# Summing the first modulation on TensorE, applying it ahead of the transposes, and writing the position bias behind the last token tile

## The chip, the cores and the metric

The kernel runs on one core of a Trainium2 chip. The metric is the device time of one execution in microseconds (us). An execution of one kernel is also taken with a hardware profiler, and every row below comes from that one profiled execution. The engines are TensorE (PE in the profile; PEld is its weight load), VectorE (DVE), ScalarE (ACT), GpSimd (POOL) and SyncE (SP), whose queue issues nearly all DMAs of this kernel.

## What is computed

One transformer layer for 1024 tokens of width 1024 in float32, with a mixer of two attention groups and a mixture of experts. The part that the change touches is the beginning of the mixer:

```python
c_act = jax.nn.silu(c)
mod = c_act @ w_ada[l] + b_ada[l]
shift_m, scale_m, gate_m, shift_f, scale_f, gate_f = jnp.split(mod, 6, axis=-1)
h = modulate(rms_norm(x), shift_m, scale_m)      # rms_norm(x) * (1 + scale_m) + shift_m
proj = h @ w_in[l]
qa, ka, va, qb, kb, vb = jnp.split(proj, ...)
qa, ka = apply_partial_rope(qa), apply_partial_rope(ka)
oa = windowed_gqa_sink(qa, ka, va, sink[l])
ob = neighbourhood_attn(qb, kb, vb, rpb[l])      # rpb: learned 2-D relative position bias
```

Everything behind it (both attentions, the output projection, the router, the experts and the final norm) is the same in both kernels.

## The kernel before, in words

All of this stands in `proj_and_a`. Tokens are worked in eight tiles of 128. A projection needs the modulated tokens with the features on the partitions, split into a high and a low part (`hh`, `hl`, fp32r) so that three matmuls (`mm3`, lines 236 to 238) give nearly float32 accuracy.

The first block (lines 336 to 404) does this:

- SyncE issues the DMAs in an order written out by hand (lines 337 to 355): the conditioning vector and the whole modulation bias into `cb`, then x tiles (`xt`, two buffers, line 350) mixed with eight blocks of `w_ada` of 1 MB each (`wa`, three buffers, line 345), the weights of keys and values (`w_chunk(512)`, whose load is line 516), the position bias (`bias_tables`, lines 655 to 664) and the rotary table `ropet` (line 355). A DMA that needs a buffer waits on SyncE until the buffer is free, and everything behind it waits too.
- `bias_tables` loads `rpb` into `erow` (line 661), negates it on POOL (line 662) and writes it 64 times over into the DRAM tensor `d_b` (line 663), whence the second attention group reads it later (line 674).
- Each x tile is squared and summed on ACT (line 366), scaled by its inverse root mean square on VectorE (line 369), transposed on TensorE (line 373) and copied by ACT into `xT` (line 375), not yet modulated.
- The modulation is summed on VectorE: for each of four column blocks, eight steps (lines 385 and 387) multiply rows of `w_ada` by the value of the conditioning vector and add them up over `acc`; TensorE then adds over the partitions (line 389), which gives scale and shift as columns `scol` (lines 392, 394).
- The modulated `hh` is written by ACT (line 399), the same in full precision by VectorE (line 400), and their difference `hl` by VectorE or POOL (line 401), in five spans of tokens, one instruction for each of eight feature blocks.
- `keys_values(i)` projects tile i onto keys and values (24 matmuls), copies them (lines 327, 329), applies the rotary table on POOL (`rope_op`, lines 533 to 536) and transposes the keys of the tile before (`k_turn`, line 317).

Behind the block come the mask (line 409), the sinks (line 411), the query weights (`w_chunk(0)`), and then query projections and windowed attention, with other projections filled in. On all engines but SyncE within this block, the order of instructions is set by a planner that places them by its own estimates of times. A tile of memory that is used again waits for the last reader of what lay there.

Of the kernel before, what the change touches and what calls it, by code (L numbers as in the profile page):

```python
# [5 lines left out]
F32 = mybir.dt.float32  # L6
# [3 lines left out]
AF = mybir.ActivationFunctionType  # L10
ALU = mybir.AluOpType
# [4 lines left out]
D = 1024  # L16
S = 1024
NT = 8
KD = 8
# [207 lines left out]
class Kernel:  # L227
# [64 lines left out]
    def proj_and_a(self):  # L292
        tc, nc = self.tc, self.nc
        V, A, P, T = nc.vector, nc.scalar, nc.gpsimd, nc.tensor
        with (
# [7 lines left out]
            scol = hp.tile([128, 16], F32, name="scol")  # L303
            ccol = hp.tile([128, 8], F32, name="ccol")
            bcol = hp.tile([128, 48], F32, name="bcol")
            self.hh, self.hl, self.kp, self.chunks = hh, hl, kp, 0
            kh = kp.tile([128, 2, S], F32R, name="kh")
            kl = kp.tile([128, 2, S], F32R, name="kl")
# [24 lines left out]
                    k_turn(i - 1)  # L333

            with tc.tile_pool(name="xp", bufs=1) as xp, tc.manual_schedule(engines={mybir.EngineType.SP}):
                cb = xp.tile([56, 128], F32, name="cb")
                nc.sync.dma_start(cb[0:8], self.c.rearrange("a (k p) -> (a k) p", p=128))
                nc.sync.dma_start(cb[8:56], self.b_ada.rearrange("a (k p) -> (a k) p", p=128))
                xt, wts = {}, {}
                for z in "0,1,w0,w1,2,w4,3,w5,4,w2,5,w3,w6,w7,6,7".split(","):  # L340
                    if z[0] == "w":
                        n = int(z[1:])
                        c, kk = divmod(n, 2)
                        w = wts[n] = xp.tile([128, 4, 512], F32, name="wa", bufs=3)
                        nc.sync.dma_start(w, self.w_ada[0, kk * 512:(kk + 1) * 512, c * 512:(c + 1) * 512]
                                          .rearrange("(k p) n -> p k n", p=128))
# [4 lines left out]
                wkv = self.w_chunk(512)  # L351
                with tc.issue_after(self.loaded):
                    self.bias_tables()
                self.ropet = kp.tile([128, NT, 32], F32, name="ropet")
                nc.sync.dma_start(self.ropet, self.rope)
                pc = ps.tile([128, 512], F32, name="pm", bufs=3)
                T.transpose(pc[:, 0:56], cb, self.idt[:56, :56])
# [3 lines left out]
                V.tensor_copy(bcol, pc[:, 8:56])  # L361
                xT = xp.tile([128, KD, S], F32, name="xT")
                for i in range(NT):
                    st = xp.tile([128, 2], F32, name="st", bufs=4)
                    junk = xp.tile([128, D], F32, name="junk", bufs=1)
                    A.activation(junk, xt[i], AF.Square, accum_out=st[:, 0:1])
                    A.activation(st[:, 1:2], st[:, 0:1], AF.Sqrt, bias=self.eps, scale=1.0 / D)
                    V.reciprocal(st[:, 1:2], st[:, 1:2])
                    V.tensor_scalar(junk, xt[i], st[:, 1:2], None, op0=ALU.mult)
                    for m in range(2):  # L370
                        pt = ps.tile([128, 512], F32, name="psc")
                        for k in range(4):
                            T.transpose(pt[:, k * 128:(k + 1) * 128], junk[:, (4 * m + k) * 128:(4 * m + k + 1) * 128],
                                        self.idt)
                        A.activation(xT[:, 4 * m:4 * m + 4, i * 128:(i + 1) * 128],
                                     pt.rearrange("p (k t) -> p k t", k=4), AF.Copy)
                pc = ps.tile([128, 512], F32, name="pm", bufs=3)
                pcv = pc[:, 0:32].rearrange("p (j t) -> p j t", t=2)
                for half in range(2):
                    for c in (half, half + 2):  # L380
                        acc = xp.tile([128, 512], F32, name="acc", bufs=2)
                        for k in range(KD):
                            w = wts[2 * c + k // 4][:, k % 4, :]
                            if k == 0:
                                V.tensor_scalar(acc, w, ccol[:, 0:1], None, op0=ALU.mult)
                            else:
                                V.scalar_tensor_tensor(acc, w, ccol[:, k:k + 1], acc, op0=ALU.mult, op1=ALU.add)
                        for j in range(4 * c, 4 * c + 4):
                            T.matmul(pc[:, 2 * j:2 * j + 2], acc[:, (j % 4) * 128:(j % 4 + 1) * 128],
                                     self.ones[:, 0:2], start=True, stop=True)  # L390
                    js = slice(4 * half, 4 * half + 4)
                    V.tensor_tensor(scol[:, js], pcv[:, js, 0], bcol[:, js], op=ALU.add)
                    js = slice(8 + 4 * half, 12 + 4 * half)
                    V.scalar_tensor_tensor(scol[:, js], pcv[:, js, 0], 1.0, bcol[:, js], op0=ALU.add, op1=ALU.add)
                for t0, t1 in ((0, 128), (128, 256), (256, 512), (512, 768), (768, 1024)):
                    for k in range(KD):
                        sl = slice(t0, t1)
                        x = xT[:, k, sl]
                        A.activation(hh[:, k, sl], x, AF.Identity, scale=scol[:, 8 + k:9 + k], bias=scol[:, k:k + 1])
                        V.tensor_scalar(x, x, scol[:, 8 + k:9 + k], scol[:, k:k + 1], op0=ALU.mult, op1=ALU.add)  # L400
                        (P if k % 4 > 1 else V).tensor_tensor(hl[:, k, sl], x, hh[:, k, sl].bitcast(F32),
                                                              op=ALU.subtract)
                    for i in range(t0 // 128, t1 // 128):
                        keys_values(i)
# [247 lines left out]

    def bias_tables(self):


        nc = self.nc
        e = self.kp.tile([120, 128], F32, name="erow", bufs=1)
# [3 lines left out]
        nc.sync.dma_start(self.d_b.rearrange("h (c m) -> h c m", m=128),  # L663
                          e.rearrange("h (c m) -> h c m", c=1).to_broadcast([120, 64, 128]))

    def tables(self, pool, h, mc, mi):

# [1076 lines left out]
```

## Time and profile before

| | |
|---|---|
| three timed runs, us | 2292.54, 2292.58, 2282.31 (median 2292.54) |
| the profiled execution's own time, us | 2281.06 |
| its span, first to last instruction, us | 2279.3 |
| mean granted TensorE clock | 0.968 |
| TensorE busy | 2083.8 us, 91% of the span |
| VectorE busy | 1593.2 us, 70% |
| ScalarE busy | 967.3 us, 42% |
| GpSimd busy | 1112.3 us, 49% |

The span is 1.8 us shorter than the time of the execution. Busy shares are means over stages with different limits. The granted clock is given as a share of full speed (2.4 GHz). A matmul's row gives its duration from issue to its modelled end; matmuls are pipelined, so the distance from one start to the next says what one costs in a row of them.

### The profile page before, as it was taken

To read this page: it belongs to the slowest core of one execution; us is meant where nothing else is said; L and a number is where in the kernel's file an instruction comes from. 1 tells how busy PE (TensorE), PEld (TensorE's weight loads), DVE (VectorE), ACT (ScalarE), POOL (GpSimd) and SP (SyncE) were. 2 spreads that over 40 slices of the span, in tenths; PEclk is the share of its full clock that TensorE was granted. 3 is DMA by queue.
4 is the path that set the end of the run, shared out by engine and by line. 5 is a ranking of instruction groups with operands and counts; after the bars stand their busy time and mean duration, and the time that the engine had idled before them with its cause. 6 is when DMAs were issued, how large, how long until landed. Compare 5 with 4: busy or idle time off the path is not lost. (4 is left out here: it accounts for less than half of the span.)

```text
span 2279.3 us, 34822 instructions
## 1 busy us (share of the span) xinstructions
PE 2083.8 (91%) x12050; PEld 1551.4 (68%) x12050; DVE 1593.2 (70%) x2860; ACT 967.3 (42%) x1650; POOL 1112.3 (49%) x970
## 2 busy tenths in 40 slices
PE   4799999999978898988979999999999999999983
PEld 4688777777767876665546555566687777877772
DVE  7577645876577599888875454455686878878864
ACT  5343335764353456554653121222233434444553
POOL 1522122543556467778784234333536455556453
PEclk9899999999988999999999999999999999999987
DMA  7755486924466698898979998999898999888775
GB/s 254 183 154 163 139 222 176 203 66 143 120 191 184 207 306 293 299 287 259 314 241 355 376 321 291 341 348 331 264 341 279 328 299 315 303 282 301 267 231 187
DMA packets 328243, 579.20 MB, mean 254 GB/s; under 512 B 40021, under 2 KB 78149, under 8 KB 326729
## 3 DMA queue, kind: packets, MB, share of 16 engines
q1 hardware_dynamic: 304657, 524.23, 67.4%
q0 software_dynamic: 23408, 52.71, 11.1%
q8 instruction: 97, 1.59, 0.3%
q14 instruction: 81, 0.66, 0.1%
HBM read 518.25 MB, written 58.92 MB: 253 GB/s over the span
## 5 line engine op out<-in xcount | busy, mean ns | idle before, releaser
L1309 POOL TENSOR_TENSOR w<-w,w 128x288 fp32r<-128x288 f32 x456 | 595.2, 1364 | 544.3 <-ACT w L1307 518.9
L1307 ACT ACTIVATE w<-w 128x1024 fp32r<-128x1024 f32 x456 | 469.6, 1054 | 517.1 <-PE accH L1536 119.3
L1309 DVE TENSOR_TENSOR w<-w,w 128x736 fp32r<-128x736 f32 x456 | 506.6, 1124 | 202.4 <-ACT w L1307 200.4
L1536 PE MATMUL accH<-xH,w 128*128 128x256 f32 (+9 forms) x1408 | 400.3, 296 | 2.7 <-POOL w L1309 1.8
L1534 PE MATMUL accH<-xH,w 128*128 128x256 f32 (+6 forms) x1024 | 322.0, 318 | 1.7 <-ACT xH L243 0.6
L1535 PE MATMUL accH<-xH,w 128*128 128x256 f32 (+6 forms) x1024 | 316.9, 311 | 0.3 <-DVE xH L244 0.3
L1536 PEld LDWEIGHTS accH<-xH,w 128*128 128x128 f32 x1408 | 272.1, 195 | 15.4 <-issue 5.0
L1534 PEld LDWEIGHTS accH<-xH,w 128*128 128x128 f32 x1024 | 194.5, 191 | 49.8 <-issue 27.3
L1535 PEld LDWEIGHTS accH<-xH,w 128*128 128x128 f32 x1024 | 195.4, 191 | 5.3 <-DVE xH L244 0.7
L1559 PE MATMUL accL<-w,xL 128*32 128x512 f32 (+3 forms) x896 | 176.9, 599 | 0.8 <-issue 0.8
L236 PE MATMUL accH<-w,hH 128*128 128x512 f32 (+3 forms) x368 | 150.0, 410 | 2.8 <-ACT w L1307 2.8
L237 PE MATMUL accH<-w,hH 128*128 128x512 f32 (+3 forms) x368 | 147.1, 400 | 0.0
L238 PE MATMUL accH<-w,hH 128*128 128x512 f32 (+3 forms) x368 | 143.0, 401 | 3.4 <-POOL w L1309 2.3
L238 PE MATMUL accL<-w,xL 128*72 128x512 f32 (+4 forms) x256 | 106.2, 415 | 38.5 <-POOL w L1309 28.4
L1532 PE MATMUL accH<-xH,w 128*128 128x416 f32 (+2 forms) x384 | 116.2, 378 | 10.7 <-DVE t L1424 10.6
L1492 POOL DMA_INDIRECT d_y<-y,lsH x54 | 96.7, 1791 | 47.3 <-DVE y L1486 33.1
L236 PE MATMUL accL<-w,xL 128*72 128x512 f32 (+4 forms) x256 | 104.0, 406 | 1.8 <-ACT w L1307 1.5
L1451 DVE TENSOR_TENSOR t<-accL,biasL 32x512 f32<-32x512 f32 (+8 forms) x88 | 60.5, 688 | 62.1 <-PE accL L1559 46.7
L237 PE MATMUL accL<-w,xL 128*72 128x512 f32 (+4 forms) x256 | 103.5, 404 | 0.0
L236 PEld LDWEIGHTS accH<-w,hH 128*128 128x128 f32 (+3 forms) x368 | 68.3, 186 | 49.9 <-issue 19.2
L1559 PEld LDWEIGHTS accL<-w,xL 128*32 128x32 f32 (+3 forms) x896 | 39.5, 115 | 84.0 <-issue 79.3
L236 PE MATMUL pm<-whi,hh 128*128 128x256 f32 x320 | 93.0, 291 | 2.4 <-DVE va L329 1.2
(362 smaller groups left out, 4477.0 us busy)
## 6 DMA issues: line engine op xcount, KB each, us to landing
w<-in_w_gate_up SPq DMA_DIRECT2D x264, 1024.0 KB
w<-in_w_down SPq DMA_DIRECT2D x132, 1024.0 KB
aw<-in_w_ada SPq DMA_DIRECT2D x64, 256.0 KB
wraw<-in_w_in SPq DMA_DIRECT2D x18, 512.0 KB
xt<-in_x SPq DMA_DIRECT2D x16, 512.0 KB
wa<-in_w_ada SPq DMA_DIRECT2D x8, 1024.0 KB
d_h<-zero SPq DMA_DIRECT2D x9, 512.0 KB
d_y<-zero SPq DMA_DIRECT2D x18, 256.0 KB
```

What stands on the lines that cost most here:

```text
L236: mm(ps, lh, rh, start=start, stop=False)
L237: mm(ps, ll, rh, start=False, stop=False)
L238: return mm(ps, lh, rl, start=False, stop=stop).ins
L1307: A.activation(hi, w, AF.Copy)
L1309: eng.tensor_tensor(lo[:, :, cs], w[:, :, cs], hi[:, :, cs].bitcast(F32), op=ALU.subtract)
L1451: V.tensor_tensor(t, p[o:o + nt], bv[o:o + nt], op=ALU.add)
L1492: s = P.indirect_dma_start(out=self.d_y[c], out_offset=bass.IndirectOffsetOnAxis(ap=b["ls"][:nt, 0:1], axis=0), in_=y, in_offset=None, com ...
L1532: mm(p[:, :2 * sp], hi[:, k, ws], x[:, :, kk, :], start=kk == 0, stop=False)
L1534: mm(p[:, :sp], hi[:, k, ws], x[:, 0, kk, :], start=kk == 0, stop=False)
L1535: mm(p[:, :sp], hi[:, k, ws], x[:, 1, kk, :], start=False, stop=False)
L1536: mm(p[:, :sp], lo[:, k, ws], x[:, 0, kk, :], start=False, stop=kk == 7)
L1559: mm(p[o:o + nt], w[:, kk, :], hi[:, k, :], start=kk < len(at), stop=kk >= 8 - len(at))
```

## The change

Four things are done, all in the first block.

- The sum of the modulation moves to TensorE. `w_ada` is loaded in eight blocks of 128 rows by 2048 columns; for each block four matmuls with the conditioning value broadcast over 32 columns add onto four 32-partition groups of one PSUM tile. The bias row is added (`rows`), and four matmuls with a broadcast column of the identity spread each 512 values over all partitions: `mod`, with 1 added to the scale.
- The modulation is applied before the transposes, on tiles with tokens on the partitions: one VectorE instruction scales by the inverse root mean square and by `mod`, and the shift is added in two halves, one on VectorE, one on POOL. The transposed PSUM tiles are split straight into `hh` and `hl`; `xT`, `scol` and `bcol` are gone. `keys_values(i)` follows each tile at once.
- x has seven buffers, h has two.
- `bias_tables` is cut in two. The load and the negation come early; the write of `d_b` is the last DMA of the block, behind x tile 7. The key weights and the rotary table come ahead of it, between x tiles 2 and 4.

```diff
-                for z in "0,1,w0,w1,2,w4,3,w5,4,w2,5,w3,w6,w7,6,7".split(","):
+                cb = xp.tile([8, 128], F32, name="cb")
+                nc.sync.dma_start(cb, self.c.rearrange("a (k p) -> (a k) p", p=128))
+                brow = xp.tile([128, 512], F32, name="brow")
+                P.memset(brow, 0.0)
+                for z in "0,w0,b,w1,w2,1,w3,w4,w5,e,2,w6,w7,p,3,r,4,5,6,7,t".split(","):
                     if z[0] == "w":
-                        n = int(z[1:])
-                        c, kk = divmod(n, 2)
-                        w = wts[n] = xp.tile([128, 4, 512], F32, name="wa", bufs=3)
...
+                        k = int(z[1:])
+                        w = wts[k] = xp.tile([128, 2048], F32, name="wa", bufs=3)
+                        nc.sync.dma_start(w, self.w_ada[0, k * 128:(k + 1) * 128, 0:2048])
+                    elif z == "b":
+                        for c in range(4):
+                            nc.sync.dma_start(brow[32 * c:32 * c + 1], self.b_ada[0:1, 512 * c:512 * c + 512])
+                    elif z in "et":
+                        self.bias_rows_b() if z == "e" else self.bias_tables()
+                    elif z == "p":
+                        wkv = self.w_chunk(512)
+                    elif z == "r":
+                        self.ropet = kp.tile([128, NT, 32], F32, name="ropet")
+                        nc.sync.dma_start(self.ropet, self.rope)
                     else:
                         i = int(z)
-                        t = xt[i] = xp.tile([128, D], F32, name="xt", bufs=2)
+                        t = xt[i] = xp.tile([128, D], F32, name="xt", bufs=NT - 1)
                         nc.sync.dma_start(t, self.x[0, i * 128:(i + 1) * 128, :])
...
+                for k in range(KD):
+                    for c in range(4):
+                        T.matmul(pc[32 * c:32 * c + 32, :], ccol[:, k:k + 1].to_broadcast([128, 32]),
+                                 wts[k][:, 512 * c:512 * c + 512], start=k == 0, stop=k == KD - 1)
+                rows = xp.tile([128, 512], F32, name="rows")
+                V.tensor_tensor(rows, pc, brow, op=ALU.add)
+                mod = xp.tile([128, 2, D], F32, name="mod")
+                for c in (2, 3, 0, 1):
+                    pc = ps.tile([128, 512], F32, name="pm", bufs=3)
+                    T.matmul(pc, self.idt[:, 32 * c:32 * c + 1].to_broadcast([128, 128]), rows, start=True, stop=True)
+                    m = mod[:, c // 2, 512 * (c % 2):512 * (c % 2) + 512]
+                    if c // 2:
+                        V.tensor_scalar(m, pc, 1.0, None, op0=ALU.add)
+                    else:
+                        A.activation(m, pc, AF.Copy)
                 for i in range(NT):
...
+                    h = xp.tile([128, D], F32, name="junk", bufs=2)
+                    A.activation(h, xt[i], AF.Square, accum_out=st[:, 0:1])
                     A.activation(st[:, 1:2], st[:, 0:1], AF.Sqrt, bias=self.eps, scale=1.0 / D)
                     V.reciprocal(st[:, 1:2], st[:, 1:2])
-                    V.tensor_scalar(junk, xt[i], st[:, 1:2], None, op0=ALU.mult)
+                    V.scalar_tensor_tensor(h, xt[i], st[:, 1:2], mod[:, 1, :], op0=ALU.mult, op1=ALU.mult)
+                    for m in range(2):
+                        cs = slice(512 * m, 512 * m + 512)
+                        (P if m else V).tensor_tensor(h[:, cs], h[:, cs], mod[:, 0, cs], op=ALU.add)
                     for m in range(2):
                         pt = ps.tile([128, 512], F32, name="psc")
                         for k in range(4):
...
-                        A.activation(xT[:, 4 * m:4 * m + 4, i * 128:(i + 1) * 128],
-                                     pt.rearrange("p (k t) -> p k t", k=4), AF.Copy)
...
+                        ks = slice(4 * m, 4 * m + 4)
+                        self.split(hh[:, ks, sl], hl[:, ks, sl], pt.rearrange("p (k t) -> p k t", k=4))
+                    keys_values(i)
```

## Rows read from the trace of the kernel before

**Rows 1.** Stages: length, busy us of each engine (x instructions), granted clock, DMA share, GB/s

```profile
30.00:40.00 10.00, 1.94 (x8) 1.57 (x8) 9.27 (x25) 7.60 (x18) 2.95 (x6) 1.00 0.87 328
...
67.00:80.50 13.50, 0.05 (x1) 0.05 (x1) 2.14 (x6) 2.21 (x5) 1.08 (x5) 0.62 0.79 184
```

**Rows 2.** Waits from 0 to 130 us: who waited for whom, us, times, longest

```profile
POOL ra L533 <- DMA ropet<-in_rope: 15.1, 1, 15.1
...
PE pt L317 <- POOL kt L536: 13.5, 1, 13.5
```

**Rows 3.** SyncE's DMA issues in order of time: start, us, line, tile

```profile
51.40 1.05 SPq L663 DMA_DIRECT2D d_b<-erow  x1
52.50 21.78 SPq L355 DMA_DIRECT2D ropet<-in_rope  x1
74.40 3.06 SPq L516 DMA_DIRECT2D wraw<-in_w_in  x2
```

**Rows 4.** All waits of TensorE from 110 to 343 us

```profile
PE pm L236 <- ACT qs L544: 1.0, 2, 0.8
```

**Rows 5.** TensorE's groups from 0 to 100 us: projection matmuls

```profile
L236 PE MATMUL pm<-whi,hh 128*128 128x256 f32 x80 | 24.0, 302 | 1.4 <-DVE va L329 1.2 <-ACT whi L243 0.2
L237 PE MATMUL pm<-whi,hl 128*128 128x256 f32 x80 | 24.0, 301 | 0.1
L238 PE MATMUL pm<-wlo,hh 128*128 128x256 f32 x80 | 23.6, 298 | 0.0
```

**Rows 6.** Groups from 0 to 130 us: the sum of the modulation on VectorE

```profile
L387 DVE SCALAR_TENSOR_TENSOR acc<-wa,ccol,acc 128x512 f32<-128x512 f32 x28 | 21.7, 777 | 0.9 <-DMA wa<-in_w_ada 0.4
```

**Rows 7.** Stages of the loads; the last number is GB/s

```profile
0.00:5.00 5.00, 0.32 (x1) 0.18 (x1) 0.51 (x4) 1.46 (x2) 0.55 (x6) 1.00 0.44 134
5.00:10.00 5.00, 0.48 (x3) 0.49 (x4) 1.04 (x3) 2.73 (x4) 0.00 (x0) 1.00 1.02 394
...
20.00:30.00 10.00, 5.37 (x24) 4.95 (x24) 8.50 (x15) 4.79 (x10) 0.00 (x0) 1.00 0.75 270
```

**Rows 8.** SyncE's waits from 0 to 200 us: x tiles for their buffers

```profile
SPq L350 <- DVE junk L369: 32.5, 6, 11.6
```

**Rows 9.** Groups of the whole run: float32 matmuls with 32 columns of weights

```profile
L1559 PE MATMUL accL<-w,xL 128*32 128x512 f32 x448 | 72.3, 602 | 0.8 <-issue 0.8
...
L648 PE MATMUL pm<-aacc,ones 128*32 128x512 f32 x16 | 8.4, 604 | 0.0
```

**Rows 10.** Groups by shape, later stages and 0 to 130 us: like operations

```profile
L1036 DVE SCALAR_TENSOR_TENSOR ya<-xt,ss,scale_f 128x1024 f32<-128x1024 f32 x8 | 10.9, 1364 | 0.5
...
L1020 DVE TENSOR_TENSOR xt<-xt,ya 128x512 f32<-128x512 f32 x8 | 6.5, 810 | 0.2
...
L244 DVE TENSOR_TENSOR xH<-pt,xH 128x512 fp32r<-128x512 f32 x36 | 23.9, 682 | 8.1 <-ACT xH L243 8.0
...
L329 DVE COPY va<-pm 128x128 f32<-128x128 f32 x8 | 2.2, 279 | 0.0
...
L244 DVE TENSOR_TENSOR kl<-pt,kh 128x256 fp32r<-128x256 f32 x8 | 3.4, 421 | 16.9 <-ACT kh L243 16.8
...
L1020 POOL TENSOR_TENSOR xt<-xt,ya 128x512 f32<-128x512 f32 x8 | 11.2, 1406 | 2.2 <-DMA xt<-in_x 1.8
...
L243 ACT ACTIVATE xH<-pt 128x512 fp32r<-128x512 f32 x4 | 2.2, 579 | 0.0
```

**Rows 11.** TensorE in order of time: start, us, line, matmuls (x how many)

```profile
9.52 1.97 PE L373 MATMUL psc<-idt,junk 128*128 128x128 f32 x8 [5.74 <-DVE junk L369]
...
52.69 0.41 PE L236 MATMUL pm<-whi,hh 128*128 128x256 f32 x1
52.90 0.41 PE L237 MATMUL pm<-whi,hl 128*128 128x256 f32 x1
...
53.40 0.28 PE L236 MATMUL pm<-whi,hh 128*128 128x256 f32 x1
53.52 0.28 PE L237 MATMUL pm<-whi,hl 128*128 128x256 f32 x1
...
54.70 1.03 PE L373 MATMUL psc<-idt,junk 128*128 128x128 f32 x8
```

More of the change, by code (lines that the diff above doesn't have):

```diff
@@ L302, in proj_and_a @@
             hl = hp.tile([128, KD, S], F32R, name="hl")
-            scol = hp.tile([128, 16], F32, name="scol")
             ccol = hp.tile([128, 8], F32, name="ccol")
-            bcol = hp.tile([128, 48], F32, name="bcol")
             self.hh, self.hl, self.kp, self.chunks = hh, hl, kp, 0
@@ L347, in proj_and_a @@
                     else:
                         i = int(z)
-                        t = xt[i] = xp.tile([128, D], F32, name="xt", bufs=2)
+                        t = xt[i] = xp.tile([128, D], F32, name="xt", bufs=NT - 1)
                         nc.sync.dma_start(t, self.x[0, i * 128:(i + 1) * 128, :])
[L351 to L354, printed above, removed]
@@ L355, in proj_and_a @@
-                nc.sync.dma_start(self.ropet, self.rope)
                 pc = ps.tile([128, 512], F32, name="pm", bufs=3)
-                T.transpose(pc[:, 0:56], cb, self.idt[:56, :56])
+                T.transpose(pc[:, 0:8], cb, self.idt[:8, :8])
                 sg = xp.tile([128, 8], F32, name="sg")
@@ L360, in proj_and_a @@
                 V.tensor_tensor(ccol, pc[:, 0:8], sg, op=ALU.mult)
-                V.tensor_copy(bcol, pc[:, 8:56])
-                xT = xp.tile([128, KD, S], F32, name="xT")
+                pc = ps.tile([128, 512], F32, name="pm", bufs=3)
[7 more added lines that the diff above has]
+                for c in (2, 3, 0, 1):
+                    pc = ps.tile([128, 512], F32, name="pm", bufs=3)
+                    T.matmul(pc, self.idt[:, 32 * c:32 * c + 1].to_broadcast([128, 128]), rows, start=True, stop=True)
[4 more added lines that the diff above has]
+                        A.activation(m, pc, AF.Copy)
                 for i in range(NT):
-                    st = xp.tile([128, 2], F32, name="st", bufs=4)
-                    junk = xp.tile([128, D], F32, name="junk", bufs=1)
-                    A.activation(junk, xt[i], AF.Square, accum_out=st[:, 0:1])
+                    sl = slice(i * 128, (i + 1) * 128)
+                    st = xp.tile([128, 2], F32, name="st", bufs=NT)
+                    h = xp.tile([128, D], F32, name="junk", bufs=2)
+                    A.activation(h, xt[i], AF.Square, accum_out=st[:, 0:1])
                     A.activation(st[:, 1:2], st[:, 0:1], AF.Sqrt, bias=self.eps, scale=1.0 / D)
                     V.reciprocal(st[:, 1:2], st[:, 1:2])
-                    V.tensor_scalar(junk, xt[i], st[:, 1:2], None, op0=ALU.mult)
+                    V.scalar_tensor_tensor(h, xt[i], st[:, 1:2], mod[:, 1, :], op0=ALU.mult, op1=ALU.mult)
+                    for m in range(2):
+                        cs = slice(512 * m, 512 * m + 512)
+                        (P if m else V).tensor_tensor(h[:, cs], h[:, cs], mod[:, 0, cs], op=ALU.add)
                     for m in range(2):
@@ L377, in proj_and_a @@
[L377 to L404, printed above, removed]
+                        ks = slice(4 * m, 4 * m + 4)
@@ L651, in ada_rest, with bias_rows_b @@
             yield
-    def bias_tables(self):
+    def bias_rows_b(self):
         nc = self.nc
-        e = self.kp.tile([120, 128], F32, name="erow", bufs=1)
+        e = self.erow = self.kp.tile([120, 128], F32, name="erow", bufs=1)
         nc.gpsimd.memset(e, 0.0)
@@ L662, in bias_tables @@
         nc.gpsimd.tensor_scalar(e, e, -1.0, None, op0=ALU.mult)
[L663 to L664 removed]
+    def bias_tables(self):
+        self.nc.sync.dma_start(self.d_b.rearrange("h (c m) -> h c m", m=128),
+                               self.erow.rearrange("h (c m) -> h c m", c=1).to_broadcast([120, 64, 128]))
     def tables(self, pool, h, mc, mi):
```

7 lines of the change are left out of this document (1 added, 6 removed).

## The prediction

> **What bounds the kernel now.** I read the stages first, then who waited for whom, then SyncE's queue. Between 67.0 and 80.5 us TensorE does nothing: 0.05 us busy in 13.5, at a mean granted clock of 0.62 [rows 1]. The waits name the cause in two steps: TensorE's key transposes wait 13.5 us for the rotary result on POOL, and POOL waits 15.1 us for the table `ropet` [rows 2]. SyncE's queue shows why such a small table is late: the position bias, 3.9 MB (120 x 64 x 128 values) in pieces of 512 bytes, is issued at 51.40, and the next DMA, the table's, occupies the queue for 21.78 us, until 74.3 [rows 3]. Nothing on that queue moves until the bias has drained. From 80.5 on TensorE does not run dry: between 110 and 343 us it waits 1.0 us in all [rows 4]. So what counts is when TensorE gets the work of this first stage behind it. My mark is the end of the eight keys-and-values tiles and the first two query projections, 10 x 24 = 240 matmuls: the three lines of `mm3` show 80 each by 100.0 us [rows 5].
>
> **The change, part by part.**
>
> *The bias write moves behind x tile 7; the table goes ahead of it.* The 13.5 us hole [rows 1] goes. Late next is what stands behind the write on SyncE: mask, sink and the query weights. Tile 7 waits for x tile 0's buffer, free after the first scaled tile (about 36.5, below), so the write is issued at about 37 and SyncE is held for 1.05 + 21.78 us [rows 3], until 60. Two weight loads take 3.06 us to issue [rows 3]; I estimate another 3 until they land, and 4 for the split (0.58 per half-tile on ACT, 2 x 1.41 on POOL [rows 10]): ready at 70. By the sum below TensorE asks at 78. The cover is 8 us; a write issued after 45 would show as a wait of TensorE on the query weights' split.
>
> *The sum leaves VectorE.* Removed are 28 multiply-adds of 0.777 us, 21.7 us in all [rows 6], four first products, and the eight plain scalings. In their place are 32 matmuls, each writing 32 columns of the array. The nearest row is a 128x512 matmul of that width: 72.3 us for 448, 0.161 each [rows 9]. Doubled for the lower clock that is 0.32, or 1.3 us for the four of one weight block, and a block of 1.05 MB takes 2.7 us at 394 GB/s [rows 7]. They hide behind the loads; without that cover 32 cost 5 to 10 us.
>
> *The loads.* All eight blocks must now land before any token is modulated. Ahead of the last are 8.39 MB of weights and three x tiles, 9.96 MB. The first 5 us moved 134 GB/s, or 0.67 MB; the other 9.3 MB take 23.6 us at 394 GB/s or 34.4 at the 270 GB/s of 20 to 30 us [rows 7]: last landing 28.6 or 39.4. I take 30, close to the fast end, because the loads of before were held by x buffers that VectorE freed late, 32.5 us of SyncE waits [rows 8], and there are now seven such buffers.
>
> *From the last block to the first scaled tile.* Four matmuls 1.3, the addition of the row 0.68 [rows 10], two broadcasts at twice 0.604 (a lone 512-column matmul [rows 9], doubled for the lower clock), one "+1" of 0.68: 30 + 1.3 + 0.7 + 2.4 + 0.7 = 35 us. The other two broadcasts run beside the first scaling.
>
> *Eight tiles.* VectorE's work per tile: scale 1.364, add half 0.810, two splits of 0.682, value copy 0.279, key split 0.421 [rows 10], reciprocal about 0.15: 4.4 us, 35.1 for eight. In 30 to 40 us VectorE was busy 9.27 of 10 [rows 1], so 37.9. The query weights' half adds 2 x 0.68 = 1.4 and the wait of the first tile on POOL, PE and ACT about 1: 35 + 37.9 + 1.4 + 1 = 75.3. POOL (1.41 for its half [rows 10] and four short rotary steps) and ACT (square and copies) need less a tile: beside it. TensorE at its upper level needs 1.03 for the transposes and 24 x 0.117 = 2.8 for the projection [rows 11]: also beside it, except the last tile.
>
> *Sum.* 75.3 + 2.8 (last projection) + 48 x 0.117 = 5.6 (two query projections): 83.7, against 100.0 [rows 5]. The gain is 16.3 us. The profiled execution took 2281.06, so 2265. The timed runs of before are 2282.31, 2292.54 and 2292.58: the profiled one stands with the lowest, and 11.5 under the median. A run in the upper group would end at 2276. VectorE without any idle time, weights at 28.6 and queries filling TensorE's gaps give some 22 to 26: 2255 to 2259.
>
> **A rule against it.** TensorE's row: eight transposes standing alone at 9.52 take 1.97 us; in the middle of dense work at 54.70 they take 1.03 [rows 11]. The Trainium skill, page "TensorE: Matmul & The Clock Gate", section "Loop structure matters more than you think", warns of exactly the new shape: a wait for a DMA between matmuls leaves TensorE at its lower clock. For the sum of the modulation I priced that level already. For the token tiles it is the third rival.
>
> **The rivals.**
> 1. *The weights land late* (0.12). If the loads keep the 270 GB/s of rows 7, everything is 9.4 us later: 2274. For: only three block buffers, each freed by matmuls. Against: the stretch at 394.
> 2. *The hole only moves* (0.08): the bias write holds the query weights as it held the table. Issued 18 us later than I think, they are ready at 88, the mark is 93.6, the gain 6: 2275. Against: 8 us of cover.
> 3. *Slower: TensorE stays at 1.2 GHz through the tiles* (0.06). Matmuls then start 0.21 us apart, not 0.12 [rows 11]: 1.97 + 24 x 0.21 + 0.7 for keys = 7.8 us a tile, 62 for eight from about 40, and 48 x 0.21 = 10 more: 112, 12 after the mark of before: 2293. It decides from (100 - 10 - 40) / 8 = 6.2 us a tile. For: tiles come one by one from VectorE, every 4.4 us, after a stage with almost no matmuls. Against: at that level TensorE would be the busiest engine, and rows 11 show the spacing fall from 0.21 to 0.12 at 53.4, in dense matmuls.
> 4. *The gain is swallowed later* (0.08). If a later stage is set by its weight loads and these do not start earlier, the time stays near 2281. Against: TensorE waits for nothing to 343 [rows 4], and buffers come free as it goes.
>
> That the bias write does not move cannot be: SyncE's order in this block is written by hand.
>
> **How the numbers follow.** My forecast, 2265, has 0.66. I take 0.5%, 11.4 us, as what a measurement of this kernel can tell from no change. Faster by more: nearly all of the forecast and part of the first rival, 0.70. Within: the rest of rivals 1 and 2, rival 4, forecasts cut short: 0.22. Slower: rival 3 and a little of 4 in the upper group of runs, 0.08. The range, 2255 to 2284, runs from the gain without idle time to a gain of 8 us in the upper group, and takes in rivals 1, 2 and 4.
>
> **What would show it.** In the changed profile: no wait of POOL on `ropet`; the bias write issued near 37 us and SyncE held for 22 behind it, with TensorE at work meanwhile; the last `wa` matmul near 31, the first scaled tile near 36; VectorE over 90% busy from 36 to 75; 240 matmuls of `mm3` by 84. Wrong would be: TensorE waiting on the query weights' split (rival 2), a first scaled tile after 42 (rival 1), matmuls 0.21 us apart after 50 (rival 3), or the mark met and the end unmoved (rival 4).

## The result, and the profile after

The changed kernel takes 2270.3 us, median of six runs, beside 2292.6 us for the kernel before in runs of the same chip. The ratio, estimated from all these runs, is 0.9923, 95% interval 0.9900 to 0.9946, or 17.7 us of the time before; the two medians alone differ by 22.3 us. The runs of each kernel spread over 10 to 14 us. The profiled executions differ by less: 2269.7 after, 2281.1 before, 11.3 us.

The stages of the changed kernel, read as [rows 1] and [rows 7] are (columns: stretch and length, busy us of PE, PEld, DVE, ACT and POOL with instructions, granted clock, DMA share, GB/s):

```profile
5.00:10.00 5.00, 1.94 (x8) 0.23 (x8) 0.16 (x1) 2.73 (x4) 0.00 (x0) 1.00 1.02 426
...
20.00:30.00 10.00, 6.82 (x32) 0.60 (x24) 0.00 (x0) 0.54 (x1) 0.55 (x1) 0.50 1.03 397
...
40.00:50.00 10.00, 9.20 (x64) 8.77 (x63) 6.67 (x11) 5.81 (x12) 2.97 (x6) 0.83 0.92 196
50.00:60.00 10.00, 9.73 (x79) 9.00 (x77) 9.72 (x17) 6.80 (x16) 5.73 (x11) 1.00 0.84 173
...
67.00:80.50 13.50, 12.71 (x107) 12.21 (x106) 11.37 (x14) 5.81 (x12) 7.82 (x14) 1.00 0.46 125
```

The hole is gone: TensorE is busy 12.71 us of the 13.5 in which it did 0.05 [rows 1]. The loads run at about 400 GB/s from 5 to 30 us, where [rows 7] fell to 270 between 20 and 30. With only the sum to do, TensorE is at its lower level of 1.2 GHz from 20 to 30 us (0.50), and it is at 2.4 GHz throughout only from 50 on. That is no cost against the kernel before. Ahead of a profile's first entry of the clock the rows show 1.00, but the matmuls there take as long as at 0.50: the four of a weight block 1.94 us between 5 and 10 us and at 27.98 alike. In the kernel before, eight lone transposes take 1.97 us and matmuls start 0.21 us apart until 53.4 [rows 11], so TensorE was at its lower level there until then.

SyncE's DMA issues, as in [rows 3]:

```profile
24.56 0.43 SPq L354 DMA_DIRECT2D ropet<-in_rope  x1
...
31.89 2.96 SPq L511 DMA_DIRECT2D wraw<-in_w_in  x2
36.64 0.34 SPq L358 DMA_DIRECT2D xt<-in_x  x1
37.03 1.06 SPq L661 DMA_DIRECT2D d_b<-erow  x1
38.13 21.65 SPq L404 DMA_DIRECT2D mask<-in_mask_a  x1
59.83 1.77 SPq L406 DMA_DIRECT2D sinkb<-in_sink  x1
71.26 0.81 SPq L633 DMA_DIRECT2D aw<-in_w_ada  x2
```

The write is issued at 37.03, 14 us earlier than before, and now the mask is the DMA that is held, 21.65 us. The query weights (31.89) went *ahead* of the write: by hand they stand behind the block, but the planner put them in front of the last x tile. SyncE is free at 61.6 us; before it was free at 78.5. The next loads, `aw` (weights of the later modulation), are issued at 71.26; in the kernel before this row reads:

```profile
87.34 0.80 SPq L638 DMA_DIRECT2D aw<-in_w_ada  x2
```

TensorE and VectorE at the start of the first tile, in order of time:

```profile
27.98 1.94 PE L367 MATMUL pm<-wa,ccol 128*32 128x512 f32 x8 [0.61 <-DMA wa<-in_w_ada]
30.78 5.74 PE L375 MATMUL pm<-rows,idt 128*128 128x512 f32 x8 [0.87 <-DVE rows L370]
...
43.90 0.41 PE L237 MATMUL pm<-whi,hl 128*128 128x256 f32 x1
44.11 0.41 PE L238 MATMUL pm<-wlo,hh 128*128 128x256 f32 x1
...
45.88 0.28 PE L236 MATMUL pm<-whi,hh 128*128 128x256 f32 x1
45.99 0.28 PE L237 MATMUL pm<-whi,hl 128*128 128x256 f32 x1
```

```profile
30.04 0.69 DVE L370 TENSOR_TENSOR rows<-pm,brow 128x512 f32<-128x512 f32 x1 [14.48 <-PE pm L367]
...
35.33 2.48 DVE L388 SCALAR_TENSOR_TENSOR junk<-xt,st,mod 128x1024 f32<-128x1024 f32 x2
```

The sum ends at 29.9, the first scaled tile starts at 35.33, and the spacing of the matmuls falls from 0.21 to 0.117 us at 45. The 240 matmuls of `mm3` are done by 82.3 us; before it was 100.0 [rows 5].

**Where the gain is later.** The last matmul of the windowed attention (`po<-th`) starts at 351.7, before at 363.9. The mark came 17.7 us earlier (that the time gives the same figure is chance); here 12.2 are left. Most of what was lost shows in TensorE's waits between the two points, 6.1 us in all, where before had 2.0 (1.0 of it in [rows 4]). The largest of them:

```profile
PE pm L643 <- DVE aacc L637: 2.6, 2, 2.3
PE psc L575 <- DVE q L555: 1.4, 1, 1.4
PE psc L575 <- DVE sm L577: 1.1, 1, 1.1
```

TensorE is now ahead of VectorE, which has the later modulation (`aacc`) to sum in the same stretch. Behind the windowed attention the distance is 14.5 us at the first matmul of the output projection, 5.0 at 1990 us in the experts, and 11.3 at the end. That stage alone varies by some 6 us between two profiles of one kernel (below), and the timed runs of the kernel before lie between 2275 and 2303 us, so only what lies ahead of 364 us can be read to 1 or 2 us.

### The profile page after: what moved, and what is told of

It reads as the page before. It is cut to its first block, busy times and chain, and to the rows that moved or that the text cites. A ratio compares the mean times of both kernels' runs of the same rounds, so it can differ in the third digit from the quotient of the medians.

```text
span 2268.0 us, 34804 instructions
## 1 busy us (share of the span) xinstructions
PE 2084.2 (92%) x12090; PEld 1533.8 (68%) x12090; DVE 1568.2 (69%) x2790; ACT 949.6 (42%) x1612; POOL 1111.3 (49%) x959
## 5 line engine op out<-in xcount | busy, mean ns | idle before, releaser
L1534 PEld LDWEIGHTS accH<-xH,w 128*128 128x128 f32 x1408 | 267.0, 191 | 18.3 <-POOL w L1307 4.8
L1532 PEld LDWEIGHTS accH<-xH,w 128*128 128x128 f32 x1024 | 193.0, 189 | 50.5 <-issue 27.4
L1533 PEld LDWEIGHTS accH<-xH,w 128*128 128x128 f32 x1024 | 193.7, 189 | 5.1 <-DVE xH L244 0.7
L238 PE MATMUL accL<-w,xL 128*72 128x512 f32 (+4 forms) x256 | 106.5, 416 | 39.9 <-POOL w L1307 28.6
L1530 PE MATMUL accH<-xH,w 128*128 128x416 f32 (+2 forms) x384 | 110.6, 365 | 10.1 <-DVE t L1422 10.0
L1449 DVE TENSOR_TENSOR t<-accL,biasL 32x512 f32<-32x512 f32 (+8 forms) x88 | 60.5, 688 | 64.2 <-PE accL L1557 45.4
L237 PE MATMUL pm<-whi,hl 128*128 128x256 f32 x320 | 92.5, 290 | 1.4 <-DVE hl L244 1.2
```

The lines of the kernel that those rows point to most:

```text
L237: mm(ps, ll, rh, start=False, stop=False)
L238: return mm(ps, lh, rl, start=False, stop=stop).ins
L1449: V.tensor_tensor(t, p[o:o + nt], bv[o:o + nt], op=ALU.add)
L1530: mm(p[:, :2 * sp], hi[:, k, ws], x[:, :, kk, :], start=kk == 0, stop=False)
L1532: mm(p[:, :sp], hi[:, k, ws], x[:, 0, kk, :], start=kk == 0, stop=False)
L1533: mm(p[:, :sp], hi[:, k, ws], x[:, 1, kk, :], start=False, stop=False)
```

## The experiments

Three numbers are given for each kernel: the ratio of its time to that of before (with its 95% interval), the mark, and the lead at the last `po<-th` matmul. The lead is counted from 364.8 us, the mean of two profiles of before (363.9 and 365.7). 1% of the time is 23 us.

| kernel | ratio | mark | lead |
|---|---|---|---|
| before, again | 1.0005 (0.9981–1.0029) | 100.0 | −0.9 |
| after | 0.9923 (0.9900–0.9946) | 82.3 | 13.1 |
| after, again | 0.9933 (0.9907–0.9959) | 83.7 | 12.1 |
| table first | 0.9971 (0.9947–0.9996) | 90.7 | 4.9 |
| table and query weights first | 0.9996 (0.9975–1.0017) | 94.7 | 1.3 |
| early write, sum on VectorE | 0.9972 (0.9946–0.9997) | 89.1 | 2.7 |
| late write, sum on TensorE | 0.9989 (0.9965–1.0014) | 94.6 | 0.5 |
| table behind the write | 0.9934 (0.9909–0.9958) | 91.2 | 5.8 |
| sum doubled | 0.9894 (0.9863–0.9924) | 90.3 | 7.3 |
| weights first | 0.9901 (0.9866–0.9936) | 82.3 | 14.1 |
| bias row in one DMA | 0.9887 (0.9851–0.9924) | 78.8 | 16.7 |
| both of these | 0.9911 (0.9889–0.9934) | 81.0 | 16.9 |
| bias in four DMAs, else before | 0.9970 (0.9954–0.9986) | 100.6 | −1.6 |

### Does the order of the queue do it alone?

The kernel before, with the table loaded ahead of the write:

```diff
                 wkv = self.w_chunk(512)
-                with tc.issue_after(self.loaded):
-                    self.bias_tables()
                 self.ropet = kp.tile([128, NT, 32], F32, name="ropet")
                 nc.sync.dma_start(self.ropet, self.rope)
+                with tc.issue_after(self.loaded):
+                    self.bias_tables()
```

> The kernel before, with one swap on SyncE's queue: the rotary table's load ahead of the position bias; the sum of the modulation stays on VectorE. Theory (the hole is the table held behind the bias write): POOL no longer waits 15 us for the table, TensorE's 13.5 us hole closes, the 240 projection matmuls are done at 86 to 89 us instead of 100.0, and the time falls by 9 to 13 us. Rival A (the hole only moves: the query weights, issued at 74, are late instead): TensorE idle 6 us or more before the first query projection, the mark at 93 or later, the time down by 3 to 6 us. Rival B (the gain of the change comes from the modulation on TensorE, the table alone is worth nothing): within 3 us of the kernel before.

The wait of POOL on `ropet` disappears, but the mark comes at 90.7, not at 86 to 89, and the time falls by 6.6 us, not by 9 to 13; 4.9 us of lead are left. SyncE's queue shows what is held now, and TensorE's largest wait from 55 us to the mark what comes of it:

```profile
51.24 1.04 SPq L663 DMA_DIRECT2D d_b<-erow  x1
52.39 23.65 SPq L516 DMA_DIRECT2D wraw<-in_w_in  x2
```

```profile
PE pt L317 <- DVE kl L244: 4.2, 1, 4.2
```

The query weights wait some 21 us behind the write. VectorE then stands 7.3 us at their split, the key split `kl` is queued behind it, and TensorE waits 4.2 us for `kl`: the second rival of the prediction, which did not come true in the changed kernel, comes true here, though milder than rival A above. So the weights were put ahead as well (the two lines of `bias_tables` moved behind the load of the query weights):

> The kernel before with order changed and nothing else: the rotary table and the query weights are issued ahead of the bias write. It tells what order alone can give. Theory: with the table early the hole is gone, and with the query weights early the wait that took its place in the first swap (mark at 90.7 there) is gone too: the mark at 85 to 88, the time down by 10 to 14 us. Rival (order alone gives no more than the first swap; the rest needs the sum off VectorE): the mark at 90 or later, the time down by 3 to 7 us.

Worse than theory and rival: 0.9996, with the mark at 94.7. The write slips to 59.41, and the next victim is the mask, and behind it the loads of the later modulation. SyncE's queue, and the stage in which TensorE stands:

```profile
59.41 1.04 SPq L663 DMA_DIRECT2D d_b<-erow  x1
60.57 21.06 SPq L407 DMA_DIRECT2D mask<-in_mask_a  x1
```

```profile
80.00:90.00 10.00, 3.50 (x28) 3.29 (x27) 1.77 (x4) 0.65 (x2) 1.78 (x7) 0.75 0.79 211
```

What is put ahead of the write makes the write itself later (59.41, where it was 51.24), and what still stands behind it is later in turn. Reordering the queue alone brings 1 and 7 us in these two kernels.

### The change with a late write

The changed kernel, with two x buffers instead of seven, so that x tiles, and the write behind them, wait for buffers again:

```diff
-                for z in "0,w0,b,w1,w2,1,w3,w4,w5,e,2,w6,w7,p,3,r,4,5,6,7,t".split(","):
+                for z in "0,w0,b,w1,w2,1,w3,w4,w5,e,w6,w7,p,r,2,3,4,5,6,7,t".split(","):
...
-                        t = xt[i] = xp.tile([128, D], F32, name="xt", bufs=NT - 1)
+                        t = xt[i] = xp.tile([128, D], F32, name="xt", bufs=2)
```

> The changed kernel with two x buffers instead of seven, as before; weights, table and all else as changed, x tiles 2 to 7 behind the key weights and the table. Each x load then waits for the scaled tile two before it, and the bias write, last of the block, is issued at about 58 us instead of 37. Theory (it is the early issue of the write that gives it cover; what stands behind it, down to the loads of the later modulation, must be let go before TensorE's queue needs it): SyncE is held to 80 or later, VectorE waits for the later modulation's weights with the key split queued behind, TensorE idles 4 us or more between 80 and 100, the mark is at 86 to 92 and the last windowed-attention matmul at 356 or later (352 in the changed kernel). Rival (the buffers only feed the tiles and the write has slack anyway): mark within 2 us of 83, the end of windowed attention within 2 us of 352.

The gain is gone (0.9989, an interval from 8 us faster to 3 us slower; lead 0.5, mark 94.6). SyncE's queue, VectorE in order of time, TensorE's largest wait, and the stage:

```profile
60.56 1.06 SPq L661 DMA_DIRECT2D d_b<-erow  x1
61.66 22.42 SPq L404 DMA_DIRECT2D mask<-in_mask_a  x1
...
86.06 1.36 SPq L633 DMA_DIRECT2D aw<-in_w_ada  x2
```

```profile
89.42 0.49 DVE L635 TENSOR_SCALAR aacc<-aw,ccol 128x512 f32<-128x512 f32 x1 [13.21 <-DMA aw<-in_w_ada]
89.82 0.42 DVE L244 TENSOR_TENSOR kl<-pt,kh 128x256 fp32r<-128x256 f32 x1
```

```profile
PE pt L315 <- DVE kl L244: 10.9, 1, 10.9
```

```profile
80.00:90.00 10.00, 0.00 (x0) 0.00 (x0) 0.58 (x2) 0.00 (x0) 0.00 (x0) 0.68 0.68 164
```

Read as a chain: write at 60.56, SyncE held to 84, `aw` issued at 86; VectorE stands 13.21 us at the first `aacc`, which needs `aw`; `kl`, a key split, is queued behind it on VectorE; TensorE waits 10.9 us for `kl` and does nothing from 80 to 90. To 80 us TensorE is about as busy as in the changed kernel (9.45 us between 70 and 80, there 9.66). So without the early write the summing on TensorE brings nothing that these runs can tell from noise.

### The kernel before with an early write

The converse: the sum stays on VectorE and x keeps its two buffers, but the key weights, the table and the write go ahead of x tile 7; the bias rows are loaded and negated earlier still (`e`).

```diff
-                for z in "0,1,w0,w1,2,w4,3,w5,4,w2,5,w3,w6,w7,6,7".split(","):
+                for z in "0,1,w0,w1,2,w4,3,w5,4,w2,5,w3,e,w6,w7,6,p,r,t,7".split(","):
...
```

> The kernel before, its sum still on VectorE and its two x buffers kept, but the key weights, the rotary table and the write of the bias placed ahead of x tile 7 (the load and negation of the bias rows earlier still). Theory 1, the instant at which SyncE reaches the write is what the gain hangs on: the write is issued near 33 us and SyncE is free by about 57, tile 7 comes some 14 us late but the query weights and the loads of the later modulation come in time; TensorE has no wait of over 4 us between 50 and 100; the 240 matmuls are done by 82 to 88, the last windowed-attention matmul starts by 356, the ratio is 0.993 to 0.996. Theory 2, the early write pays only with the sum on TensorE: with VectorE still summing, tile 7's late landing is not made up, the last two tiles wait; the mark is at 90 or later, the last windowed-attention matmul at 359 or later, the ratio 0.997 or more.

The second theory is the nearer one: 0.9972 and a last matmul at 362.1 (lead 2.7) are as it says, but the mark, 89.1, falls between the two. SyncE's queue, its wait for `aw` here and in the changed kernel, TensorE's largest wait from 55 us on, and ACT in order of time:

```profile
36.06 1.05 SPq L668 DMA_DIRECT2D d_b<-erow  x1
43.16 16.21 SPq L357 DMA_DIRECT2D xt<-in_x  x1
...
79.16 0.80 SPq L640 DMA_DIRECT2D aw<-in_w_ada  x2
```

```profile
SPq L640 <- POOL kt L538: 15.3, 1, 15.3
...
SPq L633 <- DVE junk L391: 9.5, 1, 9.5
```

```profile
PE pm L236 <- ACT qs L546: 4.8, 2, 2.8
```

```profile
95.56 1.06 ACT L243 ACTIVATE whi<-wraw 128x1024 fp32r<-128x1024 f32 x1 [6.24 <-DMA wraw<-in_w_in]
...
96.79 0.37 ACT L546 ACTIVATE qs<-pm 128x256 f32<-128x256 f32 x1
```

The write goes out at 36 and SyncE is free by 64. But the next load, `aw`, goes to memory that the first block used, and waits 15.3 us for its last user, to 79.16 (the profile names POOL's `kt`; the step just ahead of it on POOL is the block's last `hl`, which reads `xT` and ends at 79.14). In the changed kernel the same wait is 9.5 us, to 71.26, for the last half add of the shift. The weights of the next projections stand behind `aw`; ACT waits 6.24 us for them, and the copy `qs`, which frees TensorE's PSUM tile, is queued behind. Between 80 and 110 us TensorE is busy 22.6 us, in the changed kernel 28.6: the lead of the mark is lost there. So two gates stand on SyncE's queue: the 22 us of the write, and the end of the first block, whose memory the next loads need. The change opens both. The late write, which leaves the first gate shut, brings 2.5 us, and the early write with a late end of the block 6.4.

How much of the late end is VectorE's summing and how much is tile 7, which the write itself holds 16.21 us here, this run does not separate. The kernel with the table first gives a hint. There VectorE sums too, and tile 7 is not held. The block's last `hl`, first there and then here:

```profile
74.49 0.75 POOL L401 TENSOR_TENSOR hl<-xT,hh 128x256 fp32r<-128x256 f32 x1
...
78.39 0.75 POOL L403 TENSOR_TENSOR hl<-xT,hh 128x256 fp32r<-128x256 f32 x1
```

So of the 7.9 us by which `aw` goes out later here than in the changed kernel, about half seems to be tile 7's: an estimate from these rows. Seven buffers without the sum on TensorE were not run, and what the sum is worth by itself is not shown.

### The parts of the sum

The table put back behind the write in the changed kernel:

```diff
-                for z in "0,w0,b,w1,w2,1,w3,w4,w5,e,2,w6,w7,p,3,r,4,5,6,7,t".split(","):
+                for z in "0,w0,b,w1,w2,1,w3,w4,w5,e,2,w6,w7,p,3,4,5,6,7,t,r".split(","):
```

> The changed kernel with the table's load put back behind the bias write; everything else as changed. Theory: the write holds SyncE from 38 to 60 us, the table lands at about 62, TensorE's first key transposes stand in front of the other tiles' matmuls and wait some 12 to 14 us; the 240 matmuls are done at 94 to 97 instead of 82, and the time is 10 to 14 us over the changed kernel. Rival (modulation on TensorE carries the gain): under 4 us over the changed kernel.

About half of the mark's gain is lost: 91.2, where 94 to 97 were expected. POOL waits 9.0 us for `ropet`, and TensorE does 3.46 us between 60 and 70:

```profile
60.00:70.00 10.00, 3.46 (x20) 3.46 (x20) 3.27 (x6) 2.27 (x6) 4.33 (x13) 0.66 0.26 64
```

The lead falls to 5.8, but the time, 0.9934, is not measurably above the changed kernel's, where 10 to 14 us were expected. By the time alone, then, the table's place is not shown to matter in the changed kernel. The sum of the modulation doubled, by 32 more matmuls that add zeros, moves the first scaled tile from 35.3 to 42.2:

```diff
-                                 wts[k][:, 512 * c:512 * c + 512], start=k == 0, stop=k == KD - 1)
+                                 wts[k][:, 512 * c:512 * c + 512], start=k == 0, stop=False)
+                for k in range(KD):
+                    for c in range(4):
+                        T.matmul(pc[32 * c:32 * c + 32, :], self.zero[:, 0:32],
+                                 wts[KD - 1][:, 512 * c:512 * c + 512], start=False, stop=k == KD - 1)
```

> The changed kernel with the sum doubled: 32 more matmuls with zeros for weights add nothing onto the sum, between the last weight block and the row. It measures how much of a later start reaches the end. They cost 8 us at the upper clock (0.24 each) to 15 us at the lower (0.48 each), on the chain. Theory 1 (the lead passes through): the mark moves from 82 by that much and the time by the same, within 3 us. Theory 2 (the stages of the experts, paced by their weights, swallow part of a lead): the time moves by half of it or less.

The first scaled tile moves by 6.9 us and the mark by 8.0, to 90.3, and the lead falls to 7.3; but the time does not rise (0.9894), so the first theory fails on the time. (The order of the experts' stage changed too, as told below.) At last, the weights of the modulation loaded ahead of all x tiles but one:

```diff
-                for z in "0,w0,b,w1,w2,1,w3,w4,w5,e,2,w6,w7,p,3,r,4,5,6,7,t".split(","):
+                for z in "w0,b,w1,w2,0,w3,w4,w5,w6,w7,1,e,p,r,2,3,4,5,6,7,t".split(","):
```

> The changed kernel with two of the three x tiles and the bias row's source moved behind the eight weight blocks on SyncE's queue. Ahead of the last block are then 8.9 MB instead of 10.0: at 400 GB/s it lands 2.6 us earlier, if the three block buffers don't hold the queue. Theory: the first scaled tile and the mark come 2 to 3 us earlier and the time falls by 1 to 3 us. Rival (three buffers hold the loads once no x tile stands between them): the last block lands no earlier, no change.

The sum ends 0.7 us earlier (at 29.2), not 2.6, and mark and lead stay. The DMA engines were already busy throughout (share 1.0 from 5 to 28 us in both kernels, at about 400 GB/s), and SyncE waits 10.0 us for matmuls to free the three block buffers (9.2 in the changed kernel); which of the two decides is not separated.

### What else differs

In the three kernels just told, the time gains more over before than the lead at 364 us (15 to 24 us against 6 to 14). To see whether that is noise, both kernels were run again. (The stretch of 1877.7 and 1879.2 us in the two expectations ends at the experts' last matmul of line 236, not at the end of the kernel.)

> The kernel before, word for word, for a second profile. It tells how far the stages of one kernel vary from execution to execution. Theory (the front of the kernel repeats, the experts' stage varies): the 240 projection matmuls by 100.0 and the last windowed-attention matmul at 363.9 again, within 1 us; the stretch from there to the end, 1877.7 us in the first profile, differs by up to 10. Rival (all of it repeats within 2 us): then the differences between the profiles seen so far belong to the kernels.

> The changed kernel, word for word, for a second profile and more timed runs. Theory: the mark at 82.3 and the last windowed-attention matmul at 351.7 again, within 1 us; the rest, 1879.2 us in the first profile, differs by up to 10. The ratio of the times stays within 0.990 to 0.9946.

Both repeat their ratio. The front repeats a little less well than expected: the end of windowed attention moves by 1.8 us in the kernel before and by 1.0 in the changed one, whose mark moves by 1.4. And from the last `po<-th` matmul to the end the two profiles of before take 1915.4 and 1921.4 us, those of after 1916.3 and 1922.2: the later stages alone move by 6 us. Another thought was the number of SyncE's DMAs, three more in the changed kernel. The bias row by one DMA takes them away there:

```diff
-                        for c in range(4):
-                            nc.sync.dma_start(brow[32 * c:32 * c + 1], self.b_ada[0:1, 512 * c:512 * c + 512])
+                        nc.sync.dma_start(brow[0:128:32], self.b_ada[0:1, 0:2048].rearrange("a (c n) -> (a c) n", c=4))
```

> The changed kernel with the modulation's bias loaded by one DMA instead of four, so that the program has as many DMAs on SyncE's queue as the kernel before; the order of instructions on all engines is otherwise that of the changed kernel. DMAs take their completion semaphores in turn, eight of them, so three more DMAs at the front shift that turn for the whole program. Theory A (the turn means nothing, as all later DMAs shift alike): the time of the changed kernel, within 5 us. Theory B (the shift is what makes the stages behind the first 350 us about 10 us shorter in the changed kernel and its variants than in the kernel before): about 10 us over the changed kernel.

And the bias by four DMAs adds them in the kernel before:

```diff
-                nc.sync.dma_start(cb[8:56], self.b_ada.rearrange("a (k p) -> (a k) p", p=128))
+                for n in range(4):
+                    nc.sync.dma_start(cb[8 + 12 * n:20 + 12 * n],
+                                      self.b_ada.rearrange("a (k p) -> (a k) p", p=128)[12 * n:12 * n + 12])
```

> The kernel before with its modulation bias loaded by four DMAs instead of one. The front of the program keeps its order; the planner puts the experts' stage into another order, the one that the late-start kernel had, whose time fell by more than its lead at the end of windowed attention. Theory (that order is worth it): 5 to 15 us under the kernel before with the mark at 100 and windowed attention ending at 364 to 366. Rival (the order of the experts' stage is worth nothing): within 4 us of the kernel before.

The first, with the same order on every engine, is not slower but at 0.9887, with a mark of 78.8. The second is faster by 7 us at an unchanged front; yet the planner also put the experts' instructions in another order there, the one that the doubled sum has too. So some 7 us of the doubled sum's 24 can be the experts' order; that the count of DMAs matters is not seen. The two edits of the changed kernel that looked best, weights first and the bias row in one DMA, were run together:

> The changed kernel with the weights ahead of two of the x tiles and the bias row in one DMA. Theory (the mark follows the last weight block and the tiles): the mark at 76 to 80, the last windowed-attention matmul at 346 to 349, the time 3 to 6 us under the changed kernel. Rival (the waits behind 90 us swallow it): the end of windowed attention at 351 or later and the time of the changed kernel.

0.9911, with the mark at 81.0 (76 to 80 expected) and the end of windowed attention at 347.9, as expected. The intervals of these variants overlap with the changed kernel's: none is shown to beat it.

**What stays open**: why the changed kernel and its variants, with a lead of 6 to 17 us, gain 15 to 26 us in time, where the kernels with a late write or with the sum on VectorE gain within 4 us of their lead (the bias in four DMAs apart). Noise can be part of it: only for the table behind the write (10 to 21 us by its interval, lead 5.8) and the doubled sum (17 to 31, lead 7.3) does the interval lie well clear of the lead. The rest arises behind 364 us. From the output projection on, the instructions stand in the same order in all of them, but for three pairs on TensorE in some and for the doubled sum and the bias in four DMAs, and the cause was not found. So the account above is shown for the lead at 364 us; the time agrees with it in the changed kernel, but not in each of its variants.

## Why the prediction was right, and where not

The forecast said 2265 within 2255 to 2284, faster; 2270.3 came. The 2265 was reckoned from the profiled execution of before (2281.06); from the median of its timed runs the same gain of 16.3 us would give 2276. That the time came so near is in part luck, as the steps show:

- *The hole goes.* Right: TensorE is busy 12.71 of the 13.5 us of [rows 1], and POOL has no wait for `ropet` as in [rows 2].
- *"Late next is mask, sink and the query weights", with 8 us of cover.* Wrong in what is late. The forecast took SyncE's order to be written by hand; the planner issued the query weights at 31.89, ahead of the write, and TensorE never waits for their split. The 8 us of cover were thus never called on. The time of the write was right (37.03 against 37), and that it decides was right too, but through other loads: the `aw` weights and those of the next projections, as the late write shows. A write at 60 costs nearly all of the gain.
- *The sum.* The four matmuls of a block took 1.94 us, not 1.3, so one costs 0.48, not 0.32. The forecast took a record for a matmul: the profile keeps two records for each of these (x8 for the four above, x16 in [rows 9] for the eight matmuls of line 648), so the 0.161 was the cost of half of one. It did no harm: hidden behind the loads as expected, the sum ends at 29.9 (forecast 31.3).
- *To the first scaled tile.* 35.33 against 35, by two errors that cancel: the sum ended earlier, and the first two broadcasts took 3.8 us, from 30.78 to the second "+1" at 34.60, where 2.4 were put down, by the same reading of records as matmuls (5.74 for all four).
- *Eight tiles at 4.4 us.* VectorE's groups up to 100 us:

```profile
L244 DVE TENSOR_TENSOR hl<-psc,hh 128x512 fp32r<-128x512 f32 x16 | 10.8, 681 | 2.9 <-ACT hh L243 2.9
...
L388 DVE SCALAR_TENSOR_TENSOR junk<-xt,st,mod 128x1024 f32<-128x1024 f32 x8 | 10.4, 1312 | 1.0 <-issue 0.5
L391 DVE TENSOR_TENSOR junk<-junk,mod 128x512 f32<-128x512 f32 x8 | 10.3, 1292 | 0.0
```

  All prices of one instruction hold but one: the half add was put at 0.810 and takes 1.292, 3.9 us more for eight. VectorE's last split of a tile ends at 75.1, where 75.3 was forecast, again by errors that cancel. From 35.3 to 75.1 VectorE is busy 34.0 us (35.1 forecast). The dear adds are made up for by instructions that overlap at their ends (the first scaling takes 1.285 us, the next starts 1.202 after it) and by a few short steps that fall outside this stretch. It is idle 5.8 us, half of it waiting for ACT's `hh`, where 5.2 were allowed for idle time, the query weights and the first wait. So VectorE was 85% busy from 36 to 75 us, not over 90%: this sign of the forecast failed.
- *The mark.* 82.3 and 83.7 in two profiles, forecast 83.7: right, with the errors above cancelling.
- *TensorE at its lower level (rival 3).* It was there in the stretch of the sum (0.50 from 18 to 34 us), rose with the broadcasts (1.00 from 36 to 41), was there again at the first tile's matmuls after a wait of 3.0 us for VectorE (0.50 from 42 to 45), and left that level at about 45, in dense matmuls, as in [rows 11]. (The rival's sum gives 7.7 us a tile, not 7.8; nothing hangs on it.) The Trainium skill, page "TensorE: Matmul & The Clock Gate", section "Loop structure matters more than you think", warns of waits for DMAs between matmuls; the trace agrees for the loads from 20 to 30 us (0.50 granted, with waits of 0.6 to 1.9 us for `wa`), and the tiles behind it were not affected from 50 on (1.00).
- *The gain reaches the end.* This is the step that was too simple. "TensorE waits for nothing to 343" [rows 4] was true of a TensorE that came late. 18 us earlier it meets VectorE's `aacc` and its work on queries and scores, and 4 to 6 us are given back by 352. The profiled execution's gain is 11.3 us, where the mark forecast 16.3; the timed runs, with 17.7, gain more, which belongs to the point left open above.

## What to carry to other kernels

The write of 3.9 MB in pieces of 512 bytes held what stood behind it on its queue for 20 to 23 us, in every kernel here (whether by its pieces or by its size was not separated); moving the one victim ahead only picks the next. In the profile the hold stands on the DMA behind the write, not on the write (1.06 us). Ask when the queue reaches that DMA and when it is free again, and what the loads behind it wait for next: here a free queue alone brought little, since the buffers behind it were still in use, and an early end of the block alone brought nothing measurable. A stage without waits tells only that the engine is late enough for its inputs, so a gain ahead of it must be followed through the waits that it creates.

## What was not expected of the hardware

*VectorE and GpSimd slow each other.* The changed kernel adds the shift in two halves, one on each. VectorE and POOL in order of time:

```profile
51.47 0.68 DVE L391 TENSOR_TENSOR junk<-junk,mod 128x512 f32<-128x512 f32 x1
...
55.39 1.45 DVE L391 TENSOR_TENSOR junk<-junk,mod 128x512 f32<-128x512 f32 x1
```

```profile
51.28 0.25 POOL L529 TENSOR_TENSOR rb<-kt,ropet 128x32 f32<-128x32 f32 x1
51.49 0.77 POOL L530 TENSOR_TENSOR rb<-kt,ropet 128x32 f32<-128x32 f32 x1
...
55.01 1.29 POOL L391 TENSOR_TENSOR junk<-junk,mod 128x512 f32<-128x512 f32 x1 [1.22 <-DVE junk L388]
```

VectorE's add takes 0.68 us when it starts first and 1.45 when POOL's add began 0.4 us before it; and POOL's short rotary step, 0.25 us alone, takes 0.77 while VectorE's add runs. The Trainium skill, page "SBUF — State Buffer", section "SBUF: two separate sides", says that a VectorE operation with two SBUF inputs and a GpSimd operation that reads SBUF exclude each other for a whole instruction; these rows agree. The eight half adds took VectorE 10.3 us; sixteen at 0.68 would take 10.9, so giving half of the shift to POOL seems to have saved VectorE almost nothing: an estimate from these rows, as no run leaves the shift on one engine.

*The rise of the clock is not fixed.* The stretch from 40 to 50 us in the second profile of the changed kernel, and with the bias row in one DMA (the granted clock is the third number from the end; in the first profile it is 0.83, above):

```profile
40.00:50.00 10.00, 9.21 (x53) 8.77 (x52) 6.06 (x9) 4.92 (x10) 2.93 (x6) 0.66 0.90 189
...
40.00:50.00 10.00, 9.63 (x79) 9.27 (x79) 8.90 (x14) 7.40 (x16) 5.19 (x10) 1.00 0.93 208
```

In the two profiles of the changed kernel, with the same instructions, the spacing of 0.117 us sets in at 45.4 and at 48.4 us, and the mark moves from 82.3 to 83.7. With the bias row in one DMA the order on every engine is still the same, but VectorE's first add starts ahead of POOL's and takes 0.69 us (1.75 in the changed kernel, where POOL's started first). TensorE's wait before the transposes is then 1.0 us, not 3.0, the granted clock does not fall in this stretch, the spacing is 0.117 from 40.7 on, and the mark is 78.8.
